# RWKV-7 on one core: the 32-row diagonal blocks of a triangular inverse by row substitution on VectorE in place of 32-column matmuls

## The chip, the cores and the metric

One NeuronCore of a Trainium2 chip runs the whole program. The metric is the time of one execution on the device in microseconds, the median of the runs shown. TensorE is PE in the profile, its weight loads PEld, VectorE DVE, ScalarE ACT, GpSimd POOL, and SyncE SP, which here issues nearly all DMAs.

## What is computed

The network has two blocks on 256 tokens of width 2048. The second block mixes tokens in two ways, by sparse attention and by RWKV-7 with 16 heads of 64. The reference of RWKV-7 is a scan over tokens of a 64x64 state for each head:

```python
def step(state, inp):
    r_t, w_t, k_t, v_t, kk_t, a_t = inp
    sa = jnp.einsum('bhvk,bhk->bhv', state, -kk_t)
    state = (state * w_t[:, :, None, :]
             + sa[..., None] * (kk_t * a_t)[:, :, None, :]
             + v_t[..., None] * k_t[:, :, None, :])
    return state, jnp.einsum('bhvk,bhk->bhv', state, r_t)
```

The kernel works on 128 tokens of a head at a time. What the tokens of such a tile do to one another through `sa` is a strictly lower triangular 128x128 matrix N, and the tile's outputs need W = (1 - N)^-1.

## The kernel before

All products with weights go through `project` (from L178). A weight tile comes by DMA on SP's queue (`wr`, L159), is rounded to `wh` on ACT (L148), the rest `wl` is formed on DVE (L154), and three matmuls per tile follow on PE: L163 (wh with xh), L164 (wl with xh) and L165 (wh with xl), into PSUM tiles `acc`. A scheduler lays the instructions of each engine into one fixed order, and puts such products between those of other work that is emitted in the same stretch. Those other products are called filler below.

RWKV runs in two halves of 8 heads (`rwkv_half`, from L1206), each beside the projections of what comes next: the first beside the columns of sparse attention, whose index queries and keys are 296 wide, the second beside further 512-wide columns. In a half, two generators (`heads4`, one for each 4 heads, run in turn by `together`) go over two tiles of 128 tokens, t = 0 and 1. A step of one generator is: scores `psa` on PE (L1329, first all of even heads, then all of odd heads, of 64 rows each), masked on DVE to `sa` (L1331, a copy of its diagonal blocks `nd` on POOL, L1343), then W by blocks that double in size. Blocks up to 32 are kept side by side in 32 columns (`wc`), and each of the levels l = 1 to 4 is a DVE transpose of 32x32 blocks `xc` (L1352), four matmuls `pzc` (L1355), a masked spread `ztc` on DVE (L1357), four matmuls `pwc` (L1361) and an add on DVE (L1362). Levels 5 and 6 use full 128x128 tiles: transpose `px` on PE (L1369), copy `xt` on ACT (L1371), `pz` (L1375), `zt` (L1377), `pw` (L1381), add into `wt` (L1382). Then come `pk` (L1386), `pg` with W (L1395), the scores `psr` (L1329), the outputs `py` (L1412 to L1416) into `y`, and for t = 0 the state `pst`. One fp32 matmul of the program is two pieces in the trace, so 4 matmuls read x8. After a half, its heads are normed and gated on DVE (L1448 to L1466), on POOL and by PE (`pgt`, L1464); after the first half also the index scores of sparse attention are formed (L1552).

The levels below 32 are these lines:

```python
for l in range(1, 5):
    xc = tl("w", [128, 4, 32], name="xc")
    V.transpose(flat(xc), flat(wc))
    for i in range(4):
        PE.matmul(pz[:, i], nd[:, i], xc[:, i], start=True, stop=True)
    V.tensor_tensor(wide(zt), pz[:, :, None, :].to_broadcast([128, 4, 4, 32]), wide(bc4(lev[:, l * 128:(l + 1) * 128])), op=AL.mult)
    for i in range(4):
        PE.matmul(pw[:, i], zt[:, i], wc[:, i], start=True, stop=True)
    V.tensor_tensor(wc, pw, wc, op=AL.add)
```

Of the kernel before, what the change touches and what calls it, by code (L numbers as in the profile page):

```python
# [12 lines left out]
AL = mybir.AluOpType  # L13
# [4 lines left out]
D = 2048  # L18
# [36 lines left out]
def tile_kernel(ctx: ExitStack, tc: tile.TileContext, I: dict, out: bass.AP):  # L55
# [9 lines left out]
              "c": {"g": (1024, 9), "m": (512, 12), "l": (512, 3), "w": (128, 6), "f": (512, 7), "rp": (256, 2), "c": (512, 1)},  # L65
# [104 lines left out]
    class XT:  # L170
        """x transposed, in two parts: pieces of four k-tiles, [128, 4, 256] each."""
# [10 lines left out]
    def project(x, w, c0, ncols, evac, korder=None, cw=512, w_k0=0, cbs=None, feed=None, lead=2, late=0, early=0):  # L182
        """evac(cb, t, acc) for each block of columns and each tile of tokens; feed makes x, two k-tiles at a step.
        late: the first tile of tokens is finished so many steps before the second, in the last block;
        early: the second is begun so many steps after the first, in the first block."""
# [43 lines left out]
    # transposes of two k-tiles for all tokens: src(t, kt) gives [128 tokens, 128]  # L229
# [13 lines left out]
    def store_affine(x, kt, pt, scale, bias, ts=(0, 1), scratch="h"):  # L243
        """scale(kt), bias(kt): columns [128, 1]."""
# [9 lines left out]
    def affine_steps(x, src, scale, bias, scratch="h"):  # L254
        """x from src, two k-tiles at a step; the first four k-tiles tile by tile of tokens."""
# [5 lines left out]
    # (v * scale + eps)^-1/2: a first guess from the bits, then Newton; v: [128, n]  # L261
# [22 lines left out]
    # the same for one column: a first guess by log and exp, of v * 2^-46 to stay in the log's range, then Newton  # L284
# [55 lines left out]
    def ada_block_v(t0, nt, kind):  # L340
        """the same on the vector engine."""
# [1494 lines left out]
```

## Time and profile before

| what | value |
|---|---|
| runs | 2661.46, 2662.31 and 2678.67 us |
| median | 2662.31 us |
| profiled execution, span of all engines | 2664.4 us (no time but the span is given for it) |
| RWKV, scores of the first half to outputs of the second | about 1347 to 1720 us of the span |
| PE busy | 2522.0 us, 95% |
| mean DMA traffic | 181 GB/s |

Busy time is of one engine, and engines run beside one another. PE works through a queue, so a piece of a matmul can start while the last pieces of the one ahead still drain: durations of neighbours overlap, and the step from one start to the next tells what a piece costs. Granted clock 1.00 is 2.4 GHz of TensorE, 0.50 is 1.2 GHz. PE's clock is granted in full in nearly the whole span, with its lowest slice (0.6) at 1332 to 1399 us.

### The profile page before, as it was taken

The numbers are of one execution on the slowest core, as the hardware profiler recorded it, in microseconds if no ns is written. First come the engines' busy times: TensorE is split into PE (matmuls) and PEld (weight loads), VectorE is DVE, ScalarE is ACT, GpSimd is POOL, SyncE is SP. The second block draws the span as 40 slices with busy tenths as digits, with TensorE's granted clock in tenths as the row PEclk, the third lists the DMA queues.
The fourth block names the chain that finished last, engine by engine and source line by source line (L and its number), as shares of the span: only waits on it lengthen the run. The fifth ranks groups of instructions, "written<-read, shape, count | busy, mean of one in ns | idle before, by whom it ended". The sixth has DMA issues, their size and how long they took to land.

```text
span 2664.4 us, 33688 instructions
## 1 busy us (share of the span) xinstructions
PE 2522.0 (95%) x12095; PEld 2046.6 (77%) x12095; DVE 1814.0 (68%) x2960; ACT 1164.6 (44%) x1552; POOL 260.0 (10%) x213
## 2 busy tenths in 40 slices
PE   7889999889889899998999999999999999999998
PEld 5667866778677777787789778878788888888886
DVE  6799757897997877768656776675655544455544
ACT  5433244444654544436512352254554433444433
POOL 4430000220230000002010110100000000000000
PEclk9989999999999999999969999999999999999999
DMA  7767647667657777755512342135456555666664
GB/s 237 243 217 229 209 141 241 201 226 244 194 182 237 238 257 259 245 188 164 164 37 73 96 135 72 53 110 191 154 172 187 183 189 188 187 186 182 203 187 154
DMA packets 263012, 483.20 MB, mean 181 GB/s; under 512 B 20881, under 2 KB 37099, under 8 KB 262843
## 3 DMA queue, kind: packets, MB, share of 16 engines
q1 hardware_dynamic: 262523, 480.60, 57.6%
q8 instruction: 95, 1.56, 0.2%
q14 instruction: 74, 0.61, 0.1%
q10 hardware_dynamic: 320, 0.44, 0.0%
HBM read 477.82 MB, written 3.15 MB: 181 GB/s over the span
## 4 chain that ended last, share of the span: by engine, by line
PE 57%; DVE 7%; DMA 3%; ACT 1%; issue 1%; POOL 0%; SPq 0%; ACTq 0%; DVEq 0%; POOLq 0%
PE acc L163 16%; PE acc L165 16%; PE acc L164 16%; DMA ar<-in_w_ada 2%; DVE wl L154 2%; PE trp L234 1%; PE pzc L1355 1%; PE pwc L1361 1%; PE pw L1381 1%; PE pz L1375 1%; DVE aa L379 1%; PE psr L1329 0%; ACT wh L148 0%; DVE w L1344 0%; DMA lng<-in_ln_g 0%
## 5 line engine op out<-in xcount | busy, mean ns | idle before, releaser
L148 ACT CAST wh<-wr 128x1024 fp32r<-128x1024 f32 (+2 forms) x720 | 743.7, 1038 | 1044.5 <-PE acc L165 866.5
L164 PE MATMUL acc<-wl,xh 128*128 128x512 f32 (+2 forms) x2688 | 1067.5, 397 | 32.5 <-DVE wl L154 32.2
L163 PE MATMUL acc<-wh,xh 128*128 128x512 f32 (+2 forms) x2688 | 1073.8, 401 | 14.1 <-ACT xh L251 6.0
L165 PE MATMUL acc<-wh,xl 128*128 128x512 f32 (+2 forms) x2688 | 1066.5, 398 | 2.2 <-DVE xl L252 2.2
L154 DVE TENSOR_TENSOR wl<-wr,wh 128x512 fp32r<-128x512 f32 (+3 forms) x864 | 584.0, 704 | 171.4 <-ACT wh L148 170.2
L164 PEld LDWEIGHTS acc<-wl,xh 128*128 128x128 f32 x2688 | 516.5, 192 | 151.1 <-DVE wl L154 45.9
L163 PEld LDWEIGHTS acc<-wh,xh 128*128 128x128 f32 x2688 | 515.7, 192 | 131.0 <-ACT wh L148 8.1
L165 PEld LDWEIGHTS acc<-wh,xl 128*128 128x128 f32 x2688 | 516.3, 192 | 112.1 <-DVE xl L252 4.0
L151 DVE TENSOR_TENSOR wl<-wr,wh 128x1024 fp32r<-128x1024 f32 x272 | 333.2, 1225 | 357.4 <-ACT wh L148 355.4
L379 DVE SCALAR_TENSOR_TENSOR aa<-ar,cs,aa 128x512 f32<-128x512 f32 x240 | 192.0, 800 | 76.4 <-DMA ar<-in_w_ada 74.4
L355 DVE SCALAR_TENSOR_TENSOR am<-ar,cs,am 128x512 f32<-128x512 f32 (+1 forms) x150 | 109.5, 775 | 7.6 <-DMA ar<-in_w_ada 7.5
L154 POOL TENSOR_TENSOR wl<-wr,wh 128x512 fp32r<-128x512 f32 (+1 forms) x48 | 65.9, 1389 | 71.3 <-ACT wh L148 54.0
L163 PE MATMUL acc<-wh,uch 128*128 128x512 f32 x128 | 50.2, 393 | 2.5 <-DVE kc L534 2.5
L165 PE MATMUL acc<-wh,ucl 128*128 128x512 f32 x128 | 50.8, 397 | 0.0
L164 PE MATMUL acc<-wl,uch 128*128 128x512 f32 x128 | 50.8, 397 | 0.0
L1355 PEld LDWEIGHTS pzc<-xc,nd 128*128 128x128 f32 x256 | 37.0, 224 | 9.1 <-issue 8.2
L1355 PE MATMUL pzc<-xc,nd 128*128 128x32 f32 x256 | 36.6, 299 | 6.9 <-DVE xc L1352 6.9
L1361 PEld LDWEIGHTS pwc<-wc,ztc 128*128 128x128 f32 x256 | 39.3, 226 | 1.1
L701 PE MATMUL pp<-eq,ek 128*128 128x128 f32 x224 | 31.2, 294 | 8.5 <-DVE ek L713 8.5
L701 PEld LDWEIGHTS pp<-eq,ek 128*128 128x128 f32 x224 | 30.5, 209 | 11.1 <-issue 8.2
L1361 PE MATMUL pwc<-wc,ztc 128*128 128x32 f32 x256 | 37.7, 296 | 0.0
L1357 DVE TENSOR_TENSOR ztc<-pzc,lev 128x512 f32<-128x512 f32 x32 | 22.1, 692 | 21.8 <-PE pzc L1355 21.8
(568 smaller groups left out, 2408.1 us busy)
## 6 DMA issues: line engine op xcount, KB each, us to landing
ar<-in_w_ada SPq DMA_DIRECT2D x320, 256.0 KB
wr<-in_w_in_e SPq DMA_DIRECT2D x128, 512.0 KB
wr<-in_w_up SPq DMA_DIRECT2D x128, 512.0 KB
wr<-in_w_down SPq DMA_DIRECT2D x128, 512.0 KB
wr<-in_w_in SPq DMA_DIRECT2D x80, 512.0 KB
wr<-in_w_in_o SPq DMA_DIRECT2D x64, 512.0 KB
wr<-in_w_ada SPq DMA_DIRECT2D x32, 512.0 KB
wr<-in_w_out_e SPq DMA_DIRECT2D x32, 512.0 KB
```

What stands on the lines that cost most here:

```text
L148: S.copy(wh, wr)
L151: engines[0].tensor_tensor(wl, wr, wh.bitcast(F), op=AL.subtract)
L154: engines[q % 2].tensor_tensor(wl[:, q], wr[:, q], wh[:, q].bitcast(F), op=AL.subtract)
L163: PE.matmul(acc, xh, wh, start=start, stop=False)
L164: PE.matmul(acc, xh, wl, start=False, stop=False)
L165: PE.matmul(acc, xl, wh, start=False, stop=stop)
L234: PE.transpose(pt[:, q, t * 128:(t + 1) * 128], src(t, kt + q), ident)
L355: V.scalar_tensor_tensor(acc[a], w[:, q], col, acc[a], op0=AL.mult, op1=AL.add)
L379: V.scalar_tensor_tensor(acc, w, cs[:, k:k + 1], acc, op0=AL.mult, op1=AL.add)
L701: PE.matmul(pp[:, h, t], kx[:, 2 * h + c, s * 128:(s + 1) * 128], qx[:, 2 * h + c, t * 128:(t + 1) * 128], start=c == 0, stop=c == 1)
L1355: PE.matmul(pz[:, i], nd[:, i], xc[:, i], start=True, stop=True)
L1361: PE.matmul(pw[:, i], zt[:, i], wc[:, i], start=True, stop=True)
```

## The change

The diagonal 32x32 blocks of all (1 - N)^-1 of a half are found together on DVE. All scores `psa` of a half (2 tiles of tokens, 2 groups of heads) are made first and kept. POOL gathers the diagonal blocks of the 16 matrices into one tile `blk`, and a DVE transpose of 32x32 blocks puts one block in each partition (16 heads and tiles by 4 blocks is 64 partitions used). In 30 steps, column j of all rows below times row j is added to those rows: an outer product `u` (after: L1344) and an add into `inv` (after: L1345), each (31 - j) x j elements per partition. Two more transposes give W and its transposed form, and `spread` puts either into block-diagonal 128x128 tiles (`wt` and `xt`, after: L1366), so that level 5 starts without `px` and its copy. Levels 1 to 4 with `nd`, `wc`, `xc`, `pzc`, `ztc` and `pwc` go. The scores take the head's parity as innermost loop, with one PSUM tile for each parity. The tile pool of the stretch has other counts. Line numbers after L1312 shift. The core of the diff (comments that were dropped are left out):

```diff
-              "c": {"g": (1024, 9), "m": (512, 12), "l": (512, 3), "w": (128, 6), "f": (512, 7), "rp": (256, 2), "c": (512, 1)},
+              "c": {"g": (1024, 11), "m": (512, 9), "l": (512, 3), "f": (512, 7), "rp": (256, 2), "c": (512, 1)},
...
+        def scores(dst, qx_, mask, hg, t, name):
+            ps = [pside([128, 2, 2, 128], name="p" + name) for _ in range(2)]
+            for n, kx_ in enumerate((av, kx)):
+                for c in range(2):
+                    for o in range(2):
+                        PE.matmul(ps[o][:, n, c], head(kx_, hg, 2 * c + o, t), head(qx_, hg, 2 * c + o, t), start=True, stop=True)
+            for o in range(2):
+                V.tensor_tensor(dst(o).rearrange("p a b i -> p (a b) i"), ps[o].rearrange("p a b i -> p (a b) i"), bc4(mask),
+                                op=AL.mult)
+        blk = tl("g", [128, 32, 32], name="blk")
+        inv = tl("g", [128, 32, 32], name="inv")
+        G.memset(blk[:, 16:], 0.0)
+        sas = {}
+        for t in range(2):
+            for hg in range(2):
+                sa = sas[t, hg] = tl("g" if hf else "xt", [128, 2, 2, 2, 128], name="sa")
+                scores(lambda o: sa[:, o], kk, strict, hg, t, "sa")
+                b0 = (t * 2 + hg) * 4
+                for g in range(4):
+                    r = slice(g * 32, g * 32 + 32)
+                    G.tensor_copy(blk[r, b0:b0 + 4].rearrange("p (c o) i -> p o c i", o=2), sa[r, :, 0, :, r])
+        V.transpose(inv, blk.rearrange("p b i -> p i b"))
+        for j in range(1, 31):
+            n = 31 - j
+            u = tl("rp", [128, n, j], name="u")
+            V.tensor_tensor(u, inv[:, j + 1:, j:j + 1].to_broadcast([128, n, j]), inv[:, j:j + 1, :j].to_broadcast([128, n, j]), op=AL.mult)
+            V.tensor_tensor(inv[:, j + 1:, :j], inv[:, j + 1:, :j], u, op=AL.add)
+        G.memset(flat(inv)[:, ::33], 1.0)
+        invt = tl("g", [128, 32, 32], name="invt")
+        invx = tl("g", [128, 32, 32], name="invx")
+        V.transpose(invt, inv)
+        V.transpose(invx, inv.rearrange("p i j -> p j i"))
...
-                sa = scores(kk, strict, "sa")
-                nt_ = lambda i: sa[i % 2][:, 0, i // 2]
-                nd = tl("m", [128, 4, 128], name="nd")
-                w0 = tl("m", [128, 4, 128], name="w0")
-                for o in range(2):
-                    G.tensor_tensor(nd[:, o::2], sa[o][:, 0], cst[:, None, C_BD32:C_BD32 + 128].to_broadcast([128, 2, 128]), op=AL.mult)
-                    V.tensor_tensor(w0[:, o::2], sa[o][:, 0], lev[:, None, 0:128].to_broadcast([128, 2, 128]), op=AL.mult)
-                wc = tl("w", [128, 4, 32], name="wc")
-                V.tensor_reduce(wc, w0.rearrange("p h (g c) -> p h c g", c=32), axis=AX.X, op=AL.add)
...
-                for l in range(1, 5):
-                    yield
...
-                wt = tl("m", [128, 4, 128], name="wt")
-                V.tensor_tensor(wide(wt), wc[:, :, None, :].to_broadcast([128, 4, 4, 32]), wide(bc4(cst[:, C_BD32:C_BD32 + 128])), op=AL.mult)
+                sa = sas[t, hg]
+                nt_ = lambda i: sa[:, i % 2, 0, i // 2]
+                b0 = (t * 2 + hg) * 4
+                def spread(x, name):
+                    d = tl("m", [128, 4, 128], name=name)
+                    V.tensor_tensor(wide(d), x[:, :, b0:b0 + 4].rearrange("p i h -> p h i")[:, :, None, :].to_broadcast([128, 4, 4, 32]),
+                                    wide(bc4(cst[:, C_BD32:C_BD32 + 128])), op=AL.mult)
+                    return d
+                wt = spread(invt, "wt")
+                xt = spread(invx, "xt")
                 for l in range(5, 7):
                     yield
-                    px = pside([128, 4, 128], name="px")
...
+                    if l == 6:
+                        px = pside([128, 4, 128], name="px")
```

On PE, second half, level 1 before. L1355 and L1361 are the 32-column matmuls, L163 to L165 filler:

```order
L1355 MATMUL pzc<-xc,nd 128x32 x8
L165 MATMUL acc<-wh,xl 128x512
L163 MATMUL acc<-wh,xh 128x512
L164 MATMUL acc<-wl,xh 128x512
L165 MATMUL acc<-wh,xl 128x512
L1361 MATMUL pwc<-wc,ztc 128x32 x4
L163 MATMUL acc<-wh,xh 128x512
L164 MATMUL acc<-wl,xh 128x512
L1361 MATMUL pwc<-wc,ztc 128x32 x4
```

After, the first tile of tokens in the same half, from the last filler on. L1384 and L1390 are pz and pw, L1378 px, L1395 pk:

```order
L164 MATMUL acc<-wl,xh 128x512
L165 MATMUL acc<-wh,xl 128x512
L1384 MATMUL pz<-xt,sa 128x128 x8
L1390 MATMUL pw<-wt,zt 128x128 x8
L1378 MATMUL px<-cst,wt 128x128 x8
L1384 MATMUL pz<-xt,sa 128x128 x8
L1390 MATMUL pw<-wt,zt 128x128 x8
L1395 MATMUL pk<-vn,sa 128x64 x8
L1404 MATMUL pg<-rhs,wt 128x64 x8
```

The filler that lay between the matmuls of the levels now stands ahead of the first pz (160 products of 512 columns between the last psa and the first pz), and the matmuls of levels 5 and 6 follow one another with none between.

On DVE, the same place before:

```order
L1352 STREAM_TRANSPOSE xc<-wc 128x128 x2
L154 TENSOR_TENSOR wl<-wr,wh 128x512
L1357 TENSOR_TENSOR ztc<-pzc,lev 128x512 x2
L1362 TENSOR_TENSOR wc<-pwc,wc 128x128
L154 TENSOR_TENSOR wl<-wr,wh 128x512
L1362 TENSOR_TENSOR wc<-pwc,wc 128x128
```

After, in the middle of the substitution (`u` the outer product, `inv` the add, `wl` a weight's second part):

```order
L1345 TENSOR_TENSOR inv<-inv,u 128x13x18
L154 TENSOR_TENSOR wl<-wr,wh 128x512
L1344 TENSOR_TENSOR u<-inv 128x228
L1345 TENSOR_TENSOR inv<-inv,u 128x12x19
L1344 TENSOR_TENSOR u<-inv 128x220
L154 TENSOR_TENSOR wl<-wr,wh 128x512
```

The 60 operations of a half form one chain. In the first half 22 neighbours of that chain have nothing between them, in the second 36; between the others lie `wl`: 30 of 296 and 8 of 512 elements in the first half, 24 of 512 in the second.

On PE after the first half, where the index scores of sparse attention (L1552 before, L1562 after) are made, before:

```order
L1552 MATMUL pbg<-kiT,qiT 128x128 x2
L1552 MATMUL pbg<-kiT,qiT 128x256 x2
L163 MATMUL acc<-wh,xh 128x512
L164 MATMUL acc<-wl,xh 128x512
L165 MATMUL acc<-wh,xl 128x512
L163 MATMUL acc<-wh,xh 128x512
L164 MATMUL acc<-wl,xh 128x512
```

After:

```order
L163 MATMUL acc<-wh,xh 128x512
L164 MATMUL acc<-wl,xh 128x512
L165 MATMUL acc<-wh,xl 128x512
L1562 MATMUL pbg<-kiT,qiT 128x128 x2
L163 MATMUL acc<-wh,xh 128x512
L1562 MATMUL pbg<-kiT,qiT 128x128 x2
L1562 MATMUL pbg<-kiT,qiT 128x256 x8
L1562 MATMUL pbg<-kiT,qiT 128x128 x2
L164 MATMUL acc<-wl,xh 128x512
L165 MATMUL acc<-wh,xl 128x512
```

Between the first groups of these scores stood 12 products, and now one to three. Until the last `py` of the first half 86 products of 512 columns are done where 18 were, so 69 or so fewer are left behind it; in the second half 160 where 150 were.

## Rows read from the trace of the kernel before

**Rows 1.** The page, busy time of each engine (us, share of the span, instructions).
```profile
PE 2522.0 (95%) x12095; PEld 2046.6 (77%) x12095; DVE 1814.0 (68%) x2960; ACT 1164.6 (44%) x1552; POOL 260.0 (10%) x213
```
**Rows 2.** Windows: stretch, length, busy PE, PEld, DVE, ACT, POOL, granted clock, DMA share, GB/s.
```profile
1359.50:1400.00 40.50, 40.50 (x182) 40.47 (x182) 14.43 (x37) 3.43 (x5) 0.00 (x0) 0.50 0.14 39
1482.00:1530.00 48.00, 44.80 (x205) 31.31 (x205) 40.14 (x131) 21.31 (x34) 6.01 (x6) 0.96 0.34 99
1600.00:1726.00 126.00, 122.45 (x912) 110.36 (x910) 79.72 (x161) 28.62 (x45) 9.30 (x12) 0.98 0.23 66
```
**Rows 3.** The page, costliest groups: busy, mean ns of one, idle before and its releaser.
```profile
L1355 PE MATMUL pzc<-xc,nd 128*128 128x32 f32 x256 | 36.6, 299 | 6.9 <-DVE xc L1352 6.9
...
L1361 PE MATMUL pwc<-wc,ztc 128*128 128x32 f32 x256 | 37.7, 296 | 0.0
```
**Rows 4.** Timeline of PE, second half, full clock: start, duration, what.
```profile
1626.37 0.39 PE L165 MATMUL acc<-wh,xl 128*128 128x512 f32 x1
1626.60 0.97 PE L1361 MATMUL pwc<-wc,ztc 128*128 128x32 f32 x8
1627.40 0.48 PE L163 MATMUL acc<-wh,xh 128*128 128x512 f32 x1
```
**Rows 5.** Timeline of PE, first half, at the full and at the halved clock.
```profile
1358.64 0.30 PE L163 MATMUL acc<-wh,xh 128*128 128x296 f32 x1
1358.77 0.30 PE L164 MATMUL acc<-wl,xh 128*128 128x296 f32 x1
...
1366.77 0.45 PE L165 MATMUL acc<-wh,xl 128*128 128x296 f32 x1
1367.02 0.45 PE L163 MATMUL acc<-wh,xh 128*128 128x296 f32 x1
```
**Rows 6.** Timeline of PE around a transpose px of the second half.
```profile
1648.82 0.64 PE L1369 MATMUL px<-cst,wt 128*128 128x128 f32 x4
1649.29 2.00 PE L1375 MATMUL pz<-xt,sa 128*128 128x128 f32 x16
```
**Rows 7.** Window of line L1329, the scores (columns PE, PEld, clock), and a timeline of PE.
```profile
1340.00:1740.00 400.00, 26.43 (x256) 24.14 (x256) 0.92 0.27 77
...
1657.21 0.71 PE L1329 MATMUL psr<-rr,av 64*128 64x128 f32 x4
1657.76 0.27 PE L1329 MATMUL psr<-rr,rk 64*128 64x128 f32 x1
1657.77 0.37 PE L1329 MATMUL psr<-rr,av 64*128 64x128 f32 x1
1657.88 0.27 PE L1329 MATMUL psr<-rr,rk 64*128 64x128 f32 x1
```
**Rows 8.** Timeline of DVE after the first half: a dependent pair, small and 512-element operations.
```profile
1421.82 0.69 DVE L1448 TENSOR_REDUCE ymean<-y 128x8 f32<-128x512 f32 x1 [3.43 <-ACT y L1417]
1422.54 0.17 DVE L1449 TENSOR_SCALAR ymean<-ymean 128x8 f32<-128x8 f32 x1
...
1490.87 0.22 DVE L1484 TENSOR_TENSOR att<-att,rope 128x64 f32<-128x64 f32 x1
1491.00 0.16 DVE L281 SCALAR_TENSOR_TENSOR yrs<-yrst,yrs 128x8 f32<-128x8 f32 x1
...
1495.34 0.68 DVE L1461 TENSOR_TENSOR y<-y,vb 128x512 f32<-128x512 f32 x1
1495.94 0.68 DVE L154 TENSOR_TENSOR wl<-wr,wh 128x512 fp32r<-128x512 f32 x1
```
**Rows 9.** Groups by shape of DVE, 1340 to 1740 us (columns as in rows 3).
```profile
L1346 DVE TENSOR_REDUCE wc<-w 128x128 f32<-128x512 f32 x8 | 8.5, 1059 | 0.0
L1352 DVE STREAM_TRANSPOSE xc<-wc 128x128 f32<-128x128 f32 x32 | 8.3, 289 | 0.0
```
**Rows 10.** Two lines by themselves: durations in ns, least, median and longest.
```profile
L1255 DVE TENSOR_TENSOR nt<-nt,nv x6: 404/406/1497, 1326.0 to 1589.7; 8x256 f32<-8x256 f32 x6
...
L1391 POOL COPY rhs<-an x4: 396/398/403, 1460.2 to 1705.6; 128x256 f32<-128x256 f32 x4
```
**Rows 11.** Waits of PE, 1482 to 1530 us: total, times, longest.
```profile
PE pbg L1154 <- DVE att L1484: 2.0, 1, 2.0
```

More of the change, by code (lines that the diff above doesn't have):

```diff
@@ L1316, in heads4 @@
                 tok = slice(t * 128, (t + 1) * 128)
-                def head(x, i):
-                    c, o = divmod(hg * 4 + i, 2)
-                    return x[o * 64:o * 64 + 64, c, tok]
-                def scores(qx_, mask, name):
-                    res = []
-                    for o in range(2):
-                        p = pside([128, 2, 2, 128], name="p" + name)
-                        for n, kx_ in enumerate((av, kx)):
-                            for c in range(2):
-                                PE.matmul(p[:, n, c], head(kx_, 2 * c + o), head(qx_, 2 * c + o), start=True, stop=True)
-                        d = tl("m", [128, 2, 2, 128], name=name)
-                        V.tensor_tensor(d.rearrange("p a b i -> p (a b) i"), p.rearrange("p a b i -> p (a b) i"), bc4(mask),
-                                        op=AL.mult)
-                        res.append(d)
-                    return res
@@ L1336, in heads4 @@
-                hv = slice(hg * 256, hg * 256 + 256)
-                sa = scores(kk, strict, "sa")
-                nt_ = lambda i: sa[i % 2][:, 0, i // 2]
-                nd = tl("m", [128, 4, 128], name="nd")
-                w0 = tl("m", [128, 4, 128], name="w0")
-                for o in range(2):
-                    G.tensor_tensor(nd[:, o::2], sa[o][:, 0], cst[:, None, C_BD32:C_BD32 + 128].to_broadcast([128, 2, 128]), op=AL.mult)
-                    V.tensor_tensor(w0[:, o::2], sa[o][:, 0], lev[:, None, 0:128].to_broadcast([128, 2, 128]), op=AL.mult)
@@ L1345, in heads4 @@
-                wc = tl("w", [128, 4, 32], name="wc")
-                V.tensor_reduce(wc, w0.rearrange("p h (g c) -> p h c g", c=32), axis=AX.X, op=AL.add)
-                V.tensor_tensor(wc, wc, cst[:, None, C_ID32:C_ID32 + 32].to_broadcast([128, 4, 32]), op=AL.add)
-                wide = lambda x: x.rearrange("p h (g c) -> p h g c", c=32)
-                for l in range(1, 5):
-                    yield
-                    xc = tl("w", [128, 4, 32], name="xc")
-                    V.transpose(flat(xc), flat(wc))
-                    pz = pside([128, 4, 32], name="pzc")
-                    for i in range(4):
-                        PE.matmul(pz[:, i], nd[:, i], xc[:, i], start=True, stop=True)
-                    zt = tl("m", [128, 4, 128], name="ztc")
-                    V.tensor_tensor(wide(zt), pz[:, :, None, :].to_broadcast([128, 4, 4, 32]), wide(bc4(lev[:, l * 128:(l + 1) * 128])), op=AL.mult)
-                    yield
-                    pw = pside([128, 4, 32], name="pwc")
-                    for i in range(4):
-                        PE.matmul(pw[:, i], zt[:, i], wc[:, i], start=True, stop=True)
-                    V.tensor_tensor(wc, pw, wc, op=AL.add)
@@ L1365, in heads4 @@
+                wt = spread(invt, "wt")
+                xt = spread(invx, "xt")
                 for l in range(5, 7):
                     yield
-                    px = pside([128, 4, 128], name="px")
-                    for i in range(4):
-                        PE.transpose(px[:, i], wt[:, i], ident)
-                    xt = tl("m", [128, 4, 128], name="xt")
-                    S.copy(xt, px)
-                    yield
+                    if l == 6:
+                        px = pside([128, 4, 128], name="px")
+                        for i in range(4):
+                            PE.transpose(px[:, i], wt[:, i], ident)
+                        xt = tl("m", [128, 4, 128], name="xt")
+                        S.copy(xt, px)
+                        yield
@@ L1398, in heads4 @@
                 yield
-                sr = scores(rx, upto, "sr")
+                sr = [tl("m", [128, 2, 2, 128], name="sr") for _ in range(2)]
+                scores(lambda o: sr[o], rx, upto, hg, t, "sr")
                 if t:
```

6 lines of the change are left out of this document (5 added, 1 removed).

## The prediction

> **What bounds the kernel now.** I read the busy times first. PE is busy in 95% of the span, DVE in 68%, POOL in 10% [rows 1], so PE work that goes should come off the time, unless PE then waits. The windows by stage say where that can be: in the second half of RWKV PE is busy for 122.45 of 126 us with DVE at 79.72, in the stretch after the first half for 44.8 of 48 with DVE at 40.1, and in one stretch of the first half PE is busy throughout, but at a granted clock of 0.50 [rows 2]. The groups then price what goes: pzc and pwc hold PE for 36.6 and 37.7 us in 256 pieces each, and PE stood for 6.9 us before pzc, waiting for the DVE transpose xc [rows 3]. Timelines give the step from one start to the next, which is the price of a piece.
>
> **What goes from PE.** The groups' 74.3 us [rows 3] overstate pzc and pwc, since pieces overlap their neighbours. Eight pieces last 0.97 us, but the next product starts 0.80 us after them; that product then lasts 0.48 instead of 0.39 us [rows 4]. With some 52 such runs of pieces in both halves, 52 x 0.17 = 8.8 us of overlap come off, and about 45 x 0.09 = 4 us of longer products behind them come back: 70 us. The wait for xc, 6.9 us [rows 3], goes too. The px of level 5 goes in 8 groups of 8 pieces: four pieces take 0.47 us to the next start [rows 6], in level 5 as in level 6, and some lie beside other work; I take 0.5 per group, 4 us.
>
> The halved clock of the first half has PE short of nothing [rows 2], but what stood ahead of it was a wait for xc and short matmuls. A product of 296 columns steps in 0.25 us there and in 0.13 at the full clock [rows 5]. After the change only filler runs there; about 66 products of this stretch gain 0.12 each, less the part that the clock may still lose: 7 us.
>
> The scores: 256 pieces hold PE for 26.43 us, 0.103 each. Four pieces of one parity take 0.55 us to the next start, 0.1375 each; pieces of different tiles start together, a pair each 0.11 us, 0.055 each [rows 7]. If all pair, 256 x 0.055 = 14.1 us remain, so the gain lies between 0 and 12.3. I take 8, as the order alternates everywhere, but an odd piece must still wait for masks to free the two PSUM tiles.
>
> Together: 70 + 6.9 + 4 + 7 + 8 = 95.9 us.
>
> **What comes in: the substitution on DVE.** PE can't start pz before it ends. Operations of 64 elements follow each other at 0.13 us and of 512 at 0.60 [rows 8]: 0.07 us and 0.96 elements per ns. Sixty operations with 9,920 elements in sum (twice the sum of j x (31 - j)) take 4.2 + 10.3 = 14.5 us in each half. A result that the next operation reads costs more: the mean of ymean starts at 1421.82, its reader at 1422.54, 0.72 against 0.60 [rows 8], 0.125 for each of the 22 neighbours with nothing between in the first half and the 36 in the second: 2.8 and 4.5. The wl between cost 30 x 0.38 + 8 x 0.60 = 16.1 and 24 x 0.60 = 14.4. The transposes of 1024 elements take 1.14 each by the same rate (the small one, 128 elements in 289 ns with its drain, agrees [rows 9]), 3.4 us; two spreads 1.2. That is 38.0 us in either half.
>
> It begins after the last psa by the mask (0.6), four POOL copies at up to 0.40 each [rows 10] and hand-overs of about 1: 3.2 us; in the second half two more masks are queued: 4.4. Against it PE has, by the order, 58 products of 512 columns and 192 of 296 in the first half, 58 x 0.23 + 192 x 0.135 = 39.3 us [rows 4, 5], and 160 of 512 in the second, 36.8. PE waits 41.2 - 39.3 = 1.9 and 42.4 - 36.8 = 5.6 us, 7.5 in all.
>
> The Trainium skill speaks against this change in "VectorE: DVE Perf Modes", section "The TRN2 errata": each operation with SBUF sources exposes a fixed latency, many small tiles pay it each, and an fp32 tensor_tensor of N elements takes (N + 151)/0.96 ns. By that the chain would be (9,920 + 60 x 151)/0.96 ns = 19.8 us a half where the rows give 17.3 and 19.0, an estimate that would lengthen the waits by 3.3 us in all. The rows agree for dependent operations and show that independent ones hide most of it, so my sum goes by the rows.
>
> What no row shows is a read with a stride and a broadcast operand, as the two operations have. The nearest is the reduce L1346 that reads 512 elements across rows, 1.06 us [rows 9] against 0.68 for a plain operation of that size [rows 8]. The outer products have only one operand spread this way, so I take 1.2 us a half, 2.4, with bounds of 0 and 5.
>
> **Other costs.** A wait of PE may halve its clock for a while; over 48 us with waits of 2.0 and 1.2 us the granted clock was 0.96 [rows 2, 11], or 2 us lost. Two such waits: 4 us. POOL's gather and memsets lie beside filler. In the second half the tiles' matmuls now follow with no filler between: after each, PE waits for a copy or an add, and has other heads' matmuls only as cover. From the 0.47 us of px before pz can start [rows 6] I count gaps of about 1.2 us per tile: 2.5 us. DVE's work is neutral: what goes (xc 8.3, the reduce 8.5 [rows 9], and the masks and adds) is about 52 us, what comes about 50.
>
> Pulling some 69 products ahead takes cover from the stretch behind the first half. There 69 x 0.23 = 15.9 us of PE's 44.8 go, and 28.9 remain; DVE's 40.1 us less 69/6 wl of 0.6 is 33 [rows 2, 8]. The stretch becomes DVE's, and keeps 33 - 28.9 = 4 us of the gain. For SP six weight loads go ahead of the gate's loads, whose data are wanted tens of us later: nothing.
>
> Costs: 7.5 + 2.4 + 4 + 2.5 + 4 = 20.4 us. The sum is 95.9 - 20.4 = 75.5 us off the profiled 2664.4: 2588.9. That execution, known only by its span, lies 2.1 above the runs' median of 2662.3, and I forecast 2587 us for the median. With strides at 5 us and no gain from the scores it would be 2587 + 2.6 + 8 = 2598; without PE's waits, the strides and their clock (13.9) and with all scores paired (4.3) 2569.
>
> **The rivals.**
> First, the clock. If it falls to half at the wait before pz in the second half and stays there through the two tiles' matmuls, about 41 us at the full clock, a step grows as 0.25 to 0.13 [rows 5], by 0.9, so 36 us come back: 2623. For it: the clock fell in the first half after waits and short matmuls [rows 2, 5]. Against it: in the second half it stayed at 0.98 [rows 2] through many short matmuls, and 2.0 us of wait cost it little [rows 11]. The Trainium skill's "TensorE: Matmul & The Clock Gate", section "HAM oscillation", says that idle time between bursts throttles TensorE again; it would make this the result if the gaps in the bare chain are enough.
>
> Second, the feed. Filler of both halves now runs in one piece, and each weight tile must arrive, be cast on ACT and give its wl on DVE, which enters DVE's chain only where the order has put it. A chain operation that waits then holds wl, wl holds the product, and PE paces with DVE: the 38 us of DVE and the 39 of filler no longer lie beside each other but partly behind. If half of both are lost, 2 x 17 = 34 us: 2621. Against it: DMA moved 66 to 99 GB/s in these stretches [rows 2], well under the span's mean.
>
> Third, slower than before: the price of a small operation. L1255 once took 1497 ns instead of 406 [rows 10]. If the operations of the substitution took 1.2 us, for instance because POOL's copies and memsets work beside DVE, 120 x (1.2 - 0.3) = 108 us would come onto the path: 2695. It decides from a mean of 0.30 + 75.5/120 = 0.93 us. Against it: a 64-element operation stepped at 0.13 us and one of 8 elements lasted 0.16 [rows 8], and POOL did nothing in the place where the first substitution will stand [rows 2].
>
> Better than forecast: the waits are hidden, since filler runs slower than its best; then 2569.
>
> **How the numbers follow.** Forecast 0.72; the clock 0.11, the feed 0.09, slow operations 0.03, better 0.05. The range has to hold eight of ten: its lower end is the better case, less 7 us for overlap of pzc and pwc taken off too much (8.8 at most); its upper end holds the two rivals at 2621 and 2623, and 9 us for a mix. Faster by over 1% means under 2635.7; 1% is about what a measurement of this kernel can tell. The forecast, the better case and most of the two rivals lie below it: 0.91; within 1% lies the tail of these two, 0.06; slower 0.03.
>
> **What would show it.** In the profile after, pzc and pwc are gone and PE's busy time is 75 to 85 us less. The 120 operations last 0.2 to 0.45 us each. PE's wait before the first pz of a half is under 10 us. The clock reads near 1.0 at 1360 to 1400 us. The scores start in pairs. I am wrong if those operations last over 0.9 us, if the clock shows 0.5 through the second half's tiles, or if products between psa and pz step at much over 0.23 us.

## The result, and the profile after

| | before | after |
|---|---|---|
| median of the runs of one comparison | 2670.49 us (4 runs) | 2593.82 us (4 runs, 2582.51 to 2598.57) |
| span of the profiled execution | 2664.4 us | 2593.7 us |
| from the first half's `pbon` to the end | 1328.07 us | 1253.14 us |

The ratio of the times is 0.9703, with a 95% interval of 0.9651 to 0.9754: the changed kernel is faster. A second comparison, with 6 runs, gave 0.9725 (0.9685 to 0.9765) and a median of 2589.12 us. The forecast was 2587 us: 75.5 us below 2662.3, the median of the runs shown ahead of it. The kernel before scatters more than the changed one: over all comparisons its runs lie between 2639 and 2705 us, the quicker ones at the higher granted clock (0.973 to 0.976 up to 2648 us, 0.949 at 2705), while ten runs of the changed kernel lie between 2582 and 2599 us at 0.970 to 0.978.

The third row of the table needs a word, since all experiments are read by it. The first block is the same in all kernels, yet it ended between 1324 and 1342 us in the profiles, which hides differences of a few us. `pbon` (L1276) is one of the last matmuls on PE ahead of the first half's scores; from its start to the end of the span every kernel does what the change touches, and two profiles of the unaltered changed kernel gave 1253.14 and 1252.63 us there. Two profiles of another kernel (e2 and g2 below) gave 1253.03 and 1255.20 us, so differences of 2 us say nothing. Of the kernel before there is one profile.

The page after, busy times:

```profile
PE 2442.7 (94%) x11551; PEld 1970.2 (76%) x11551; DVE 1813.7 (70%) x2966; ACT 1157.8 (45%) x1542; POOL 262.1 (10%) x233
```

Against [rows 1] PE has 79.3 us less, DVE the same. The windows from `pbon` to the end (stretch, length, busy PE, PEld, DVE, ACT, POOL, granted clock, DMA share, GB/s), of before:

```profile
1336.33:2664.40 1328.07, 1296.94 (x6573) 1078.42 (x6572) 759.02 (x1214) 546.42 (x745) 46.59 (x49) 0.97 0.48 147
```

and of after, with the place that ran at the halved clock before, the stretch from the end of the first half to the second `pbon`, and a window at the second half's wait:

```profile
1340.56:2593.70 1253.14, 1214.25 (x6029) 997.62 (x6028) 757.58 (x1221) 539.59 (x735) 47.96 (x70) 0.99 0.49 156
...
1360.00:1400.00 40.00, 38.24 (x241) 34.98 (x239) 37.90 (x101) 19.11 (x28) 1.03 (x4) 1.00 0.64 189
1453.20:1551.10 97.90, 90.88 (x408) 67.01 (x407) 83.13 (x241) 50.80 (x79) 14.32 (x12) 0.98 0.37 111
1600.00:1620.00 20.00, 13.03 (x64) 10.46 (x63) 15.94 (x30) 1.86 (x3) 0.78 (x3) 0.83 0.29 87
```

PE is busy for 1296.94 - 1214.25 = 82.7 us less, and idle for 38.9 instead of 31.1 us, 7.8 more. So 82.7 - 7.8 = 74.9 us are gone. The clock at 1360 to 1400 us, 0.50 in [rows 2], is now 1.00. DVE, at 14.43 us of 40.5 there before, is now busy for 37.90 of 40: the substitution stands there.

PE's waits from `pbon` to the end (waits in us, times, longest), after:

```profile
PE pz L1384 <- DVE xt L1366: 7.8, 2, 5.1
PE pbg L1154 <- DVE att L1494: 4.4, 3, 2.1
PE acc L164 <- DVE wl L154: 2.9, 4, 1.1
PE pbg L1154 <- DVE yrst L279: 2.2, 1, 2.2
```

The wait for xc, 6.9 us [rows 3], is replaced by one for xt, 7.8 us in two pieces. The second, on PE's timeline (start, duration, what, idle before and its releaser):

```profile
1606.36 0.40 PE L165 MATMUL acc<-wh,xl 128*128 128x512 f32 x1
1611.90 3.92 PE L1384 MATMUL pz<-xt,sa 128*128 128x128 f32 x16 [5.14 <-DVE xt L1366]
1615.60 2.65 PE L1390 MATMUL pw<-wt,zt 128*128 128x128 f32 x16
...
1619.53 2.05 PE L1384 MATMUL pz<-xt,sa 128*128 128x128 f32 x16
1621.41 1.77 PE L1390 MATMUL pw<-wt,zt 128*128 128x128 f32 x13
```

Filler ends at 1606.76 and pz waits for 5.14 us. The 16 pieces then step to the next group in 3.70 us and those of level 6, 7.6 us later, in 1.88: the wait also costs 1.8 us of clock, and some 0.6 more in pw. DVE's timeline over the same place and an earlier piece of the substitution shows what PE waits for:

```profile
1571.28 2.10 DVE L1340 STREAM_TRANSPOSE inv<-blk 128x1024 f32<-128x1024 f32 x1 [1.37 <-POOL blk L1339]
1573.29 0.66 DVE L154 TENSOR_TENSOR wl<-wr,wh 128x512 fp32r<-128x512 f32 x1
...
1600.32 0.34 DVE L1345 TENSOR_TENSOR inv<-inv,u 128x184 f32<-128x184 f32 x1
1600.70 0.34 DVE L1344 TENSOR_TENSOR u<-inv 128x168 f32<-128x168 f32 x1
1601.07 0.33 DVE L1345 TENSOR_TENSOR inv<-inv,u 128x168 f32<-128x168 f32 x1
...
1606.90 1.25 DVE L1350 STREAM_TRANSPOSE invt<-inv 128x1024 f32<-128x1024 f32 x1
1608.08 1.86 DVE L1351 STREAM_TRANSPOSE invx<-inv 128x1024 f32<-128x1024 f32 x1
1609.86 0.98 DVE L1366 TENSOR_TENSOR wt<-invt,cst 128x512 f32<-128x512 f32 x1
1610.76 0.99 DVE L1366 TENSOR_TENSOR xt<-invx,cst 128x512 f32<-128x512 f32 x1
```

The chain steps from 1600.32 to 1600.70 for 184 elements, 0.38 us; by 0.07 + 184/960 + 0.125 it is 0.387. From 1573.29 to 1606.90 the chain with its 24 wl took 33.6 us, and the forecast's three terms make 14.5 + 4.5 + 14.4 = 33.4. The transposes and the spreads around it are longer than forecast where they read with a stride: 2.0 and 1.8 us to the next start against 1.2 for the plain one, and 0.9 for a spread against 0.6.

### The profile page after: what moved, and what is told of

Same layout as the page of the kernel before. It is cut to its first block, busy times and chain, and to the rows that moved or that the text cites. A ratio compares the mean times of both kernels' runs of the same rounds, so it can differ in the third digit from the quotient of the medians.

```text
span 2593.7 us, 32574 instructions
## 1 busy us (share of the span) xinstructions
PE 2442.7 (94%) x11551; PEld 1970.2 (76%) x11551; DVE 1813.7 (70%) x2966; ACT 1157.8 (45%) x1542; POOL 262.1 (10%) x233
## 4 chain that ended last, share of the span: by engine, by line
PE 54%; DVE 9%; DMA 3%; ACT 2%; issue 2%; POOL 0%; SPq 0%; ACTq 0%; DVEq 0%; POOLq 0%
PE acc L163 15%; PE acc L164 15%; PE acc L165 15%; DVE wl L154 2%; DMA ar<-in_w_ada 2%; PE trp L234 2%; PE pw L1390 1%; ACT wh L148 1%; PE pz L1384 1%; DVE aa L379 1%; DMA wr<-in_w_in 1%; DVE inv L1345 0%; PE pbg L1562 0%; DVE u L1344 0%; DMA lnb<-in_ln_b 0%
## 5 line engine op out<-in xcount | busy, mean ns | idle before, releaser
L163 PE MATMUL acc<-wh,xh 128*128 128x512 f32 (+2 forms) x2688 | 1067.6, 398 | 15.4 <-ACT xh L251 6.6
L165 PE MATMUL acc<-wh,xl 128*128 128x512 f32 (+2 forms) x2688 | 1061.7, 396 | 1.9 <-DVE xl L252 1.9
L163 PEld LDWEIGHTS acc<-wh,xh 128*128 128x128 f32 x2688 | 512.2, 191 | 129.9 <-ACT xh L251 7.7
L165 PEld LDWEIGHTS acc<-wh,xl 128*128 128x128 f32 x2688 | 513.7, 191 | 110.3 <-DVE xl L252 3.6
L163 PE MATMUL acc<-wh,uch 128*128 128x512 f32 x128 | 50.0, 392 | 2.5 <-DVE kc L534 2.5
L165 PE MATMUL acc<-wh,ucl 128*128 128x512 f32 x128 | 51.1, 399 | 0.0
L701 PEld LDWEIGHTS pp<-eq,ek 128*128 128x128 f32 x224 | 30.4, 208 | 11.3 <-issue 8.3
L326 PE MATMUL ada<-wl,c 128*4 128x512 f32 (+1 forms) x80 | 27.6, 356 | 7.9 <-DVE wl L154 7.9
L995 POOL TENSOR_TENSOR sgo<-sgo,psc 128x512 f32<-128x512 f32 x8 | 12.6, 1597 | 191.2 <-ACT sgo L989 134.2
L163 PEld LDWEIGHTS acc<-wh,uch 128*128 128x128 f32 x128 | 24.6, 192 | 8.3 <-DVE kc L534 3.0
L1799 ACT ACTIVATE un<-acc,rml 128x512 f32<-128x512 f32 x32 | 22.0, 688 | 15.6 <-PE acc L165 15.6
L431 DVE SCALAR_TENSOR_TENSOR xl<-trp,pr,xh 128x256 fp32r<-128x256 f32 x48 | 22.4, 480 | 9.4 <-ACT xh L430 9.3
```

The costliest lines, as they stand in the source:

```text
L163: PE.matmul(acc, xh, wh, start=start, stop=False)
L165: PE.matmul(acc, xl, wh, start=False, stop=stop)
L326: PE.matmul(acc, c4[:, k0 + q], wl[:, q], start=False, stop=k0 + q == 15)
L701: PE.matmul(pp[:, h, t], kx[:, 2 * h + c, s * 128:(s + 1) * 128], qx[:, 2 * h + c, t * 128:(t + 1) * 128], start=c == 0, stop=c == 1)
```

## The experiments

Theory: the change takes the 32-column matmuls and their waits off PE, some 84 us, and gives back only what PE waits for the substitution, some 14 us. Rivals: the removed matmuls lay beside waits that stay; the clock; the filler's feed; slow small operations. In the table, kernels are read from `pbon` to the end. The medians come from five comparisons, in which the kernel before had medians from 2668 to 2682 us; the last column is of one execution each.

| run | what | median us | ratio to before, interval | from pbon to the end |
|---|---|---|---|---|
| f6_before_no_levels | before, levels 1 to 4 out | 2575.31 | 0.9635, 0.9586 to 0.9685 | 1240.85 |
| f7_after_no_steps | after, no steps | 2573.40 | 0.9623, 0.9566 to 0.9680 | 1241.24 |
| e4_every_second_step | after, half of the steps | 2588.27 | 0.9657, 0.9616 to 0.9697 | 1249.25 |
| e3_outer_twice | after, 60 operations more | 2620.63 | 0.9783, 0.9744 to 0.9821 | 1285.06 |
| e2_scores_old_order | after, old order of scores | 2585.63 | 0.9658, 0.9619 to 0.9697 | 1253.03 |
| g1_changed_again | after, unaltered | 2589.12 | 0.9725, 0.9685 to 0.9765 | 1252.63 |
| g2_scores_old_order_again | as e2 | 2589.15 | 0.9725, 0.9689 to 0.9762 | 1255.20 |
| e1_before_alternating | before, scores alternate | 2682.84 | 1.0068, 1.0033 to 1.0102 | 1327.63 |
| e5_x_first | after, xt ahead of wt | 2590.09 | 0.9679, 0.9631 to 0.9728 | 1252.74 |
| f8_px_back | after, px for level 5 | 2590.49 | 0.9683, 0.9633 to 0.9732 | 1264.46 |
| f9_combined | after, three edits | 2589.13 | 0.9675, 0.9635 to 0.9716 | 1254.46 |
| h1_half_of_wl_on_pool | after, POOL forms half of wl | 2632.60 | 0.9885, 0.9832 to 0.9938 | 1283.55 |

### What the 32-column work was worth

f6_before_no_levels, of the kernel before:

```diff
-                for l in range(1, 5):
+                for l in range(1, 1):
```

> The kernel before with levels 1 to 4 left out (no xc, pzc, ztc, pwc; the inverse is incomplete). It tests the terms of the sum on what goes: 70 us of pzc and pwc, 6.9 of waits for xc, 7 of products at the halved clock, 84 in all. From the span's 2664.4 that is 2580; from the first half's pbon to the end 1328.1 becomes about 1244. Rival: these matmuls lay beside waits of the chain that stay (masks, ACT copies, DVE), and their removal only bares them: 50 to 60 us, 2605 to 2615.

The window from `pbon` to the end:

```profile
1332.55:2573.40 1240.85, 1213.44 (x6061) 996.84 (x6060) 724.23 (x1119) 546.21 (x745) 48.95 (x49) 0.99 0.50 158
```

1328.07 - 1240.85 = 87.2 us went, 83.5 of them PE's busy time. The theory said 84, the rival 50 to 60. The matmuls lay on the path nearly in full. The rival's mechanism is there, but small: at px, where PE hardly waited before, it now waits for wt eight times, 7.1 us in all, while the 6.9 us for xc are gone.

### What the substitution costs

f7_after_no_steps and e4_every_second_step, of the changed kernel, in f7

```diff
-        for j in range(1, 31):
+        for j in range(1, 1):
```

and, in e4,

```diff
-        for j in range(1, 31):
+        for j in range(1, 31, 2):
```

> The changed kernel with all 60 operations of the substitution left out in each half (gather, transposes and spreads stay; the inverse is incomplete). If what the substitution still costs is only PE's wait and the halved clock behind it, 8 to 13 us go: 2581 to 2586, from pbon to the end 1253.1 becomes 1240 to 1245. With every second step left out 3.8 went; if that is proportional, 7.6. Rival: DVE work that is off the path costs elsewhere too, since wl waits behind it: over 20 us.

> The changed kernel with every second step of the substitution left out (30 operations and about 9 us of DVE a half; the inverse is then incomplete). Theory: what the substitution costs is PE's wait behind it, so only that goes: waits of 2.7 and 5.1 us, about 4 us of halved clock behind them, 1.6 us of waits for wl: 8 to 13 us faster, 2581 to 2586. Rival: DVE bounds the halves; then the whole 19 us go, 2575.

The window of f7 from `pbon` to the end:

```profile
1326.66:2567.90 1241.24, 1212.35 (x6029) 995.90 (x6028) 723.16 (x1101) 541.80 (x737) 46.61 (x69) 0.99 0.49 157
```

PE's waits in that window:

```profile
PE pz L1384 <- DVE xt L1366: 6.6, 3, 3.1
...
PE pbg L1154 <- DVE att L1494: 0.7, 1, 0.7
```

Without any step 1253.14 - 1241.24 = 11.9 us go, inside 8 to 13, although 34 us of DVE work go. (The median, 2573.40, lies below the 2581 to 2586 that I expected; in the profile the first block ended 14 us earlier than in the changed kernel's.) Nearly all of the 11.9 us is idle time of PE: 38.9 us fall to 28.9. By place, 5.1 of these 10.0 us went in the second half, 4.0 behind it and 0.8 in and behind the first half.

In the second half PE's wait before pz fell from 5.1 to 2.9 us, and two waits for wl ahead of it, 1.6 us, went; in the first half the wait before pz rose from 2.7 to 3.6 us. The order tells why: with fewer steps the planner (the scheduler that fixes each engine's order) puts fewer products ahead of the first pz (160 in the second half, 103 with half the steps, 32 with none) and leaves the others for later. With products to spare the wait is, as I read it, what the planner misjudges; no run places pz by hand, so this is not shown. Of these three kernels only the changed one has none left in its second half between pz and the last py: there the filler has also run out. Behind the second half PE waits 4.0 us for att in the changed kernel and not at all in f7, where 102 products more are left for that place. My reason, that PE's wait at pz is what the substitution costs, holds for the amount and only in part for the place.

With half of the steps only 3.9 us go, and e4 missed the 8 to 13: its waits before pz are 3.9 and 3.5 us, and its waits for att, 6.0 in all, are longer than the changed kernel's 4.4.

f6 and f7 also set the rest of the change apart. Without the levels and without the steps the two kernels end 0.4 us apart, so levels and steps make the whole difference: 87.2 us before, 11.9 after, 75.3 saved, of 74.9 measured. What the two still differ in, namely the scores' order, the px of level 5 in the one and the gather, transposes and spreads in the other, comes to about nothing together; single terms may cancel in it.

### The scores' order

e2_scores_old_order forms the scores in the changed kernel parity by parity as before; g2_scores_old_order_again is the same kernel in a second comparison, beside g1_changed_again, the changed kernel. e1_before_alternating puts the new loop into the kernel before:

```diff
-                    for o in range(2):
-                        p = pside([128, 2, 2, 128], name="p" + name)
-                        for n, kx_ in enumerate((av, kx)):
-                            for c in range(2):
+                    ps = [pside([128, 2, 2, 128], name="p" + name) for _ in range(2)]
+                    for n, kx_ in enumerate((av, kx)):
+                        for c in range(2):
+                            for o in range(2):
```

> The changed kernel, but each parity's scores in one piece as before, with a mask after each parity. My prediction put 8 us on the alternation (0 to 12.3), so this would be 8 us slower than the changed kernel, some 2602. A rival from the profile after: line of the scores holds PE for 25.03 us against 26.43 before, so the alternation is worth 1.4 us and this kernel can't be told from the changed one (within 5 us of 2594).

> The changed kernel unaltered, beside the next two on one chip. Its time should lie between 2580 and 2600 us; from pbon of the first half to the end some 1250 to 1256 us, as in its first profile (1253.1), whatever the first block does before that.

> The changed kernel with the scores' order of before, again, beside the changed kernel. From pbon to the end it was 1253.0 against 1253.1, but its median 2585.6 against 2593.8. If the alternation is worth nothing, both medians now lie within 5 us; if the old order is better by itself, it is 5 to 10 us faster again.

> The kernel before with the scores alternating between parities and nothing else changed. By my prediction's term 8 us faster than before (0.3%), with the scores' line holding PE for some 18 us instead of 26.43. By the run with the old order in the changed kernel: no difference, the line still at 25 to 26 us, since both generators' scores already pair.

The median of e2, 2585.63, fits neither of its two expectations. From `pbon` to the end the old order gave 1253.03 us against 1253.14, and in the second comparison, side by side, 1255.20 against 1252.63, with medians of 2589.15 and 2589.12. In the kernel before the new order gave 1327.63 against 1328.07, and a ratio of 1.0068, while the runs of both kernels scatter by 40 us and more: I read no difference. The window of the scores' line (columns PE, PEld, clock, DMA share, GB/s), after and in e1:

```profile
1340.00:1740.00 400.00, 25.03 (x256) 22.02 (x256) 0.97 0.33 100
```

```profile
1340.00:1740.00 400.00, 23.63 (x256) 20.56 (x256) 0.92 0.26 78
```

The line holds PE for 1.4 to 2.8 us less than the 26.43 of [rows 7], not 8. The trace tells how far the order went: counting two pieces that start within 0.04 us as a pair, 44 of 128 possible pairs stood in the kernel before, 67 after and 82 in e1. So the new order does pair more, but not all, and a further pair saves 0.06 to 0.07 us of PE's busy time. In the time it can't be found.

### Where more is hidden, the clock gives way

e3_outer_twice, of the changed kernel: the line of the outer product stands twice.

```diff
             V.tensor_tensor(u, inv[:, j + 1:, j:j + 1].to_broadcast([128, n, j]), inv[:, j:j + 1, :j].to_broadcast([128, n, j]), op=AL.mult)
+            V.tensor_tensor(u, inv[:, j + 1:, j:j + 1].to_broadcast([128, n, j]), inv[:, j:j + 1, :j].to_broadcast([128, n, j]), op=AL.mult)
```

> The changed kernel with each outer product u formed twice: 30 more operations a half, 4,960 elements, 7.3 us by 0.07 us + 0.96 elements per ns. Theory: the end of the substitution on DVE releases PE, and in the second half no filler is left to cover more (the order has all 160 products ahead of pz), so the wait before the second half's first pz grows from 5.1 to about 12 us; in the first half the order brings 69 more products in and covers it. 8 to 14 us slower than the changed kernel, 2602 to 2608. Rival: the filler's own feed sets the time and the chain lies beside it; then within 4 us of the changed kernel, and the wait stays at 5.

It is 26.8 us slower than the changed kernel's median (2620.63 against 2593.82), far over 8 to 14, and 31.9 from `pbon` to the end. Its waits in that window show the first part:

```profile
PE pz L1385 <- DVE xt L1367: 19.8, 2, 16.2
PE pd L1217 <- DVE y L1477: 4.0, 1, 4.0
```

The wait of the second half grew from 5.1 to 16.2 us, by 11. I had said 7, since I took the second u to be free of the first. It isn't: where nothing stands between, u follows u after 0.43 us for 234 elements, with the 0.125 us of a dependent operation, though it reads nothing of it. 30 x 0.125 = 3.8 us make up the rest. The second part is in the stretch behind the first half. The order took 46 more products out of it (215 left, 261 in the changed kernel), and it grew from 97.9 to 106.5 us instead of shrinking by 46 x 0.23 = 10.6. A window inside it:

```profile
1480.00:1500.00 20.00, 17.90 (x64) 14.08 (x62) 13.23 (x39) 8.57 (x18) 0.29 (x1) 0.50 0.00 1
```

The clock was granted at half there (0.73, 0.50 and 0.75 in the three windows from 1460 to 1520 us). PE's idle time in the stretch grew from 7.0 to 12.3 us, so by difference the larger part of what was lost there is the clock's. This is my first rival, the clock, but in another place than I had put it: in the second half's bare chain the clock was full again 6.2 us after the first pz, while behind the first half it stayed at half for 34 us. It fell during PE's wait of 4.0 us for y, the second row of the waits above. The Trainium skill's "TensorE: Matmul & The Clock Gate", section "HAM oscillation", says that waits between bursts throttle TensorE again; here the rule and the row agree.

### Three attempts at the path to pz, and px

e5_x_first swaps the two transposes and the two spreads; f9_combined adds a gather that POOL writes so that the first transpose reads plainly, and the scores' old order; f8_px_back makes xt of level 5 by px again and drops invx with its spread.

```diff
-                wt = spread(invt, "wt")
-                xt = spread(invx, "xt")
+                xt = spread(invx, "xt")
+                wt = spread(invt, "wt")
...
-        V.transpose(invt, inv)
-        V.transpose(invx, inv.rearrange("p i j -> p j i"))
+        V.transpose(invx, inv.rearrange("p i j -> p j i"))
+        V.transpose(invt, inv)
...
-                    G.tensor_copy(blk[r, b0:b0 + 4].rearrange("p (c o) i -> p o c i", o=2), sa[r, :, 0, :, r])
-        V.transpose(inv, blk.rearrange("p b i -> p i b"))
+                    G.tensor_copy(blk[r, :, b0:b0 + 4].rearrange("p i (c o) -> p o c i", o=2), sa[r, :, 0, :, r])
+        V.transpose(flat(inv), flat(blk))
```

> The changed kernel with the transposed inverse (invx) made and spread (xt) before the plain one (invt, wt), since pz reads xt alone and wt is read later by pw. invt's transpose (1.25 us) and one spread (1.03) leave the path to the first pz: its wait falls by 2.3 us in each half, and 2 to 5 us of the time, 2589 to 2592, under what the runs tell apart. Rival: pw then waits for wt and takes it back: wait before pw of about 2 us, no gain.

> The changed kernel with three edits that shorten the path to the first pz: invx and xt ahead of invt and wt, the gather on POOL written so that the first transpose reads without a stride (2.09 to 1.25 us), and the scores by parity as before. Theory: the planner puts pz where it thinks that xt is ready, and its wait is what it misjudges, so PE's waits before the first pz fall from 7.8 to about 3 us and some of the halved clock goes: 3 to 8 us faster than the changed kernel, 2586 to 2591; from pbon to the end 1245 to 1250. Rival: POOL's strided writes take longer and eat it: no gain.

> The changed kernel with px on PE and the ACT copy for level 5 again, and without invx and its spread. By my sum px is worth 4 us, so 4 us slower. Rival, from the trace after: the strided transpose invx takes 1.9 us and a spread 1.0 on the path to the first pz, so about 3 us of wait go in each half for 2 us of px: 2 to 4 us faster than the changed kernel. From pbon to the end: 1257 against 1250.

e5 and f9 gained nothing: 1252.74 and 1254.46 us from `pbon` to the end, and waits before pz of 7.0 us in both, where e5 expected 2.3 us less in each half and f9 some 3 us in all. The planner knows what it has shortened and again places pz early (157 products ahead of it in the second half, 160 in the changed kernel). I read the wait as its error, which shortening the chain doesn't mend; that is argued, not shown. f8 is 11.3 us longer from `pbon` to the end, and its window shows why this says little of px:

```profile
1450.00:1480.00 30.00, 30.00 (x98) 21.47 (x97) 20.40 (x59) 12.44 (x22) 0.81 (x2) 0.54 0.22 65
```

PE's waits just ahead of it, 1400 to 1460 us:

```profile
PE pbg L1154 <- DVE yrst L279: 2.2, 1, 2.2
PE pbg L1154 <- DVE att L1490: 1.9, 1, 1.9
```

This is again the stretch behind the first half, at the halved clock; by 30 x (1 - 0.54) it cost up to 13.8 us in this execution. The two waits alone don't explain it. The changed kernel run again, g1, has the same two, 2.2 us for yrst at 1449 us and 1.9 for att at 1454, and its clock stayed full:

```profile
1448.00:1478.00 30.00, 25.58 (x130) 18.11 (x129) 28.48 (x96) 15.03 (x29) 4.19 (x5) 1.00 0.24 71
```

Nor is it a want of filler: 268 products stood in this stretch of f8 and 261 in the changed kernel's. What sent the clock down in f8 stays open. Its median, 2590.49, is level with the changed kernel's. The four us that I put on px are not confirmed; the exact price of px stays open.

### The slower rival

h1_half_of_wl_on_pool lets POOL form every other wl from the second block on:

```diff
     enter("c")
+    split_on[0] = (V, G)
```

> The changed kernel, but from the second block's first line on every other wl is formed on POOL, as in the first block's start, where one of 512 elements takes 1.63 us there. In the second half 12 of 24 wl leave DVE's chain, 7 us of it, and the order puts 139 instead of 160 products ahead of the last pz. Theory: the chain with the wl in it is the path to pz, so the wait and its halved clock shrink and the stretch behind the first half has less DVE work: 5 to 15 us faster than the changed kernel, from pbon to the end 1238 to 1248 against 1253.1. Rival: POOL beside DVE makes each small operation slower (over 0.5 us where 0.2 to 0.4 are seen), or POOL's in-order queue delays the gather behind wl: slower than the changed kernel, over 1256.

The theory, 5 to 15 us faster, failed. The kernel was slower than the changed one by 38.8 us (2632.60 against 2593.82) and by 30.4 from `pbon` to the end. One of its groups of DVE operations, 1330 to 1740 us (busy, mean ns):

```profile
L1346 DVE TENSOR_TENSOR inv<-inv,u 128x240 f32<-128x240 f32 x4 | 3.1, 777 | 0.1
```

The timelines of DVE and of POOL in the first half's substitution, and at one operation of the second half's:

```profile
1365.55 0.30 DVE L1345 TENSOR_TENSOR u<-inv 128x130 f32<-128x130 f32 x1
1365.88 0.81 DVE L1346 TENSOR_TENSOR inv<-inv,u 128x130 f32<-128x130 f32 x1
1366.72 0.95 DVE L1345 TENSOR_TENSOR u<-inv 128x150 f32<-128x150 f32 x1
1367.71 0.32 DVE L1346 TENSOR_TENSOR inv<-inv,u 128x150 f32<-128x150 f32 x1
...
1365.57 1.93 POOL L154 TENSOR_TENSOR wl<-wr,wh 128x296 fp32r<-128x296 f32 x2 [2.37 <-ACT wh L148]
...
1606.73 1.43 DVE L1345 TENSOR_TENSOR u<-inv 128x184 f32<-128x184 f32 x1
...
1606.57 1.38 POOL L154 TENSOR_TENSOR wl<-wr,wh 128x512 fp32r<-128x512 f32 x1 [1.27 <-ACT wh L148]
```

The add of 240 elements takes 0.78 us on the mean; in the changed kernel none of the 120 operations took over 0.41. Of the 120 operations 21 lasted over 0.6 us: 0.81 to 0.97 in the first half, where POOL's wl have 296 elements, and 0.74 to 1.43 in the second, where they have 512. Each of the 21 lies beside a wl on POOL and ends within 0.3 us after it. That is the mechanism of my slower rival, at a smaller size: the mean of the 120 rose from 0.33 to 0.46 us, and the rival needed 0.93. It is not all of the 30 us either. PE then waits for wl 18 times, 14.7 us, where it was 2.9, and h1 doesn't set the slow operations apart from wl that POOL delivers late. The Trainium skill's "SBUF — State Buffer", section "SBUF: two separate sides", says that a VectorE operation with two SBUF inputs and a GpSimd operation that reads SBUF take turns at one pair of ports; the rows agree. In the changed kernel POOL has 1.03 us of work in the 40 us of 1360 to 1400, so the case doesn't arise.

## Why the prediction was right, point by point

- **The sum.** 75.5 us were forecast, 70.7 lie between the spans, 74.9 between the windows from `pbon`, 76.7 between the medians. What goes was confirmed by itself: 84 us were priced for the 32-column work, 87.2 went in f6. What comes was confirmed in amount, 13.9 us for waits, strides and clock of the substitution against 11.9 in f7, and in part in place: 5.1 us of PE's idle time went in the second half, but 4.0 were waits for att behind it, which the forecast had not counted.
- **The substitution's length.** 0.07 us and 0.96 elements per ns for an operation, 0.125 for a dependent neighbour, and the wl between, gave 33.4 us for either half's chain, and 33.6 were measured in the second, 34.7 in the first. For the operations that read with a stride I took 1.2 us a half and put it on the outer products. These cost nothing extra; the transposes and spreads do, about 2.1 us a half.
- **The waits.** 7.5 us were forecast, 7.8 came, with 2 us of clock each. The amount was right and the reason half right: filler did end before the chain, in the second half because no product was left, but with shorter chains and products to spare the waits stay at 6.6 to 7.4 us in all, since, as I read it, the planner places pz by its own estimate.
- **"I take 8, as the order alternates everywhere".** This step failed: the alternation is worth about nothing in the time and 1.4 us of PE's busy time. A third of the pairs, 44 of 128, stood in the kernel before, as the rows with two starts at one time showed [rows 7], and the new order brought them to 67, not to all. The price of a single piece was too high as well: 0.1375 us takes in the slower first step of the four, and the steps behind it are 0.111. Why the rest don't pair stays open.
- **The px of level 5, 4 us, and 4 us kept by the stretch behind the first half.** The first can't be seen: the halves of f8 (110.3 and 109.3 us from `pbon` to the last py) are as long as after (112.6 and 107.6). The second was too high: that stretch shrank from 112.5 to 97.9 us, 14.6 of the 65 x 0.23 = 15.0 us of products taken out. The gains put too high (scores 8, px 4) and the saving put too low (matmuls 3, substitution 2, stretch 4) cancel in part, to 72.5 us: that the sum came so near is partly luck.
- **The halved clock of the first half.** It went, as forecast: 1.00 at 1360 to 1400. But the term of 7 us, for the filler, is not all that the sum holds of the clock. Of the 512 pieces of pzc and pwc 120 lay in that stretch, with 26.4 of the 74.3 us, 0.22 each where the others took 0.12: some 12 us of their price is the clock's, an estimate. By the mean granted clock of the two profiled executions, 0.967 and 0.974, some 18 us of the 70.7 between their spans are, also an estimate. Against the quickest runs of the kernel before, 2639 to 2648 us at 0.973 to 0.976, the change saves 50 to 60 us; no profile shows whether those lack the halved stretch.
- **The rivals.** A clock at half for some 30 us came in e3 and f8, in the stretch behind the first half, and in neither profile of the changed kernel. The feed did not pace: 189 GB/s were moved at 1360 to 1400, and PE waited 2.9 us for wl in all. (Its price of 2 x 17 us is not derived: half of 38 is 19.) The slower rival needs POOL at work beside the chain, which h1 showed at half the rival's size and the changed kernel avoids.

No version tried that forms the whole inverse beats the changed kernel by more than the runs tell apart.

## What to carry to other kernels

In this kernel, whose TensorE is busy nearly throughout, short matmuls cost what they occupied (83.5 of 87.2 us in f6), and a chain of small VectorE operations could replace them since filler lay beside it: price the chain by the step from start to start, with an extra for dependent neighbours and one for what the scheduler puts between. Then ask where the filler was taken from, since the place that gave it may be the next to wait and to lose the clock, as in e3. Ask too how much of the price was paid at a halved clock. And keep GpSimd off such work as wl while the chain runs, as h1 shows.

## What was not expected of the hardware

- Two operations that write the same tile one after the other pay the dependent step even where the second reads nothing of the first: 0.43 us for 234 elements, where 0.07 + 234/960 = 0.31 would do (e3).
- A transpose of 1024 elements on DVE takes 1.25 us when it reads plainly, 1.86 to 2.00 and 2.10 with a stride; in f9, where the gather was written so that the first one reads plainly, that one took 1.25 instead of 2.10. An outer product with broadcast operands lasts no longer than the add of its size beside it (0.34 and 0.33 us for 168 elements).
- PE can stay at the halved clock for long while it is busy throughout: 40.5 us in the first half of the kernel before [rows 2], and 30 us at 0.54 in f8. The same two waits, of 2.2 and 1.9 us, stood ahead of that stretch in f8 and at the same place in g1, where the clock was 1.00. The waits alone don't tell which it will be.
- A VectorE operation of 0.3 to 0.4 us that lies beside a GpSimd wl can last until that wl ends, 0.74 to 1.43 us (21 of 120 operations in h1).
